# How each stage of a two-layer decoder trunk opens: tile 0 first on four units or a whole chunk, weights split ahead into idle places

## The chip, the cores and the metric

The kernel runs on one core of one Trainium2 chip. The metric is the device time of one execution in microseconds (us). The core has a matrix engine (TensorE, "PE" in the profile, "PEld" for its weight loads), a vector engine (VectorE, "DVE"), a scalar engine (ScalarE, "ACT"), GpSimd ("POOL") and SyncE ("SP", which here only issues the loads of weights and inputs and the stores of the result). Each engine works through its own queue in the order in which the program wrote it, and waits on semaphores for the others. SBUF is the on-chip memory; PSUM is the small memory that TensorE accumulates into.

## The reference

A decoder trunk of two layers on 256 tokens of width 2048, in float32. Cut to what matters:

```
for layer in (0, 1):
    if layer == 0:  q, k, v = split(h @ w_qkv)          # 16 heads of 128, causal, T5 bias
    else:           k, v = split(h @ w_kv); q = h @ w_q # 4 shared K/V heads, window 128, sinks
    attn = softmax(q k^T / sqrt(128) + bias) v @ w_o
    h = layer_norm(sqrt(2) * h + attn)
    u = causal_conv3(h @ w_up) + b                      # 2 x 5504 columns
    g, v = split(u)
    h = layer_norm(sqrt(2) * h + (gelu(g) * v) @ w_down)
```

With 256 tokens the block selection of the first layer leaves plain causal attention. Nearly all the work is the products with weights: 724 weight tiles of 128 x 1024 numbers, each used once.

## The kernel before, in words

**Precision by splitting.** [...] The activations lie in SBUF already split: `xT` holds 16 blocks of 128 features, each with 256 high columns (tokens) and 256 low columns. Weights arrive as float32 ("raw", four buffers, `RAW_BUFS`), one tile of 128 x 1024 at a time, which the code calls a half. `split_upto(i)` (lines 74 to 89) splits all halves up to number i: ACT copies the raw tile to the rounded `wh` (line 85), DVE subtracts to get `wl` (line 86), and the raw buffer is reloaded with the half four further on (`load_weights`, on SP's queue, line 71). The split tiles rotate through four buffers (`spool`, `HALF_BUFS`). `take()` hands the next half to the matmuls, after it has asked for the split of the three halves ahead (`AHEAD`).

**Two ways to multiply.** In `ws_unit` (line 195) the weights are TensorE's stationary operand and all 512 columns of `xT` move: per block of 128 rows one matmul of 512 columns (line 224) and one of 256 (line 227). A unit gives 128 output features for all tokens; it uses two halves. In `Moving` (line 230) the activations are stationary and 512 weight columns move: per block and token tile three matmuls of 512 columns (lines 246 to 248). A chunk gives 512 output columns for both token tiles (tile 0 is tokens 0 to 127, tile 1 the rest).

**Stages.** First attention: V by chunks, Q and K by units, attention per head, and the projection (`project_out`, source `oT`). Then the first feed-forward: 86 units (gate and value feature tiles in turn), a convolution and gate on each pair, and the projection down (`project_out`, source `aT`, 43 blocks a chunk). Then the same for layer 1; its attention begins with one V chunk and four K units. Each `project_out` (line 287) has four chunks of 512 columns; the chunk's sums go to the residual `res` by `evac` (lines 301 and 302, two DVE operations a token tile), queued at the first `take` of the next chunk.

**A stage change.** The next stage needs the normalized residual, turned. In its last 16 blocks (the window, eight halves) a projection works tile by tile (`tilewise`, `late`): all of tile 0 first, then all of tile 1. When tile 0 is complete, DVE evacuates it, takes its moments and normalizes it in four groups of 512 columns (`norm`, lines 317 and 318, two DVE operations a group); while TensorE does tile 1, each group is transposed by TensorE (`turn`, line 327, four transposes), copied by ACT to the high half of `xT` (line 329), and its remainder is written by DVE (`low`, line 334). The window's eight halves have to stay in SBUF for both passes: four in `spool`, and four in `xT`, which is idle then (`aside`). Tile 1 is treated alike, but after the projection's end: the next stage begins meanwhile. A feed-forward begins with one `ws_unit` with `feed`, whose matmuls (lines 208, 209, 213; 256 columns each) start on a block when its turn has been done; the second attention begins with a V chunk whose first eight blocks go tile by tile (`early`).

**Order.** All engines' programs are written out in one order by hand (`manual_schedule`). `at(n, f)` puts f before the matmuls of the n-th step from now, `pe_at` behind them; a step is a half. The framework adds the semaphores.

Of the kernel before, what the change touches and what calls it, by code (L numbers as in the profile page):

```python
# [29 lines left out]
WINDOW = 128  # L30
# [12 lines left out]
WINDOW_BLOCKS = 2 * (HALF_BUFS + SPARE)  # L43


@with_exitstack
def trunk(ctx: ExitStack, tc: tile.TileContext, wst, xT_in, x_in, relb, onehot, umask, sinks, conv_in, ln_g, ln_b, out):
# [13 lines left out]
    todo = {"load": 0, "split": 0}  # L61
# [12 lines left out]
    def split_upto(i):  # L74
        while todo["split"] <= min(i, n_halves - 1):
            s = todo["split"]
            r = raws.pop(s)
            if s in aside:
                j = aside.pop(s)
                wh, wl = (xT[:, k:k + 2, :].rearrange("p a b -> p (a b)") for k in (4 * j, 4 * j + 2))  # L80
            else:
                wh = spool.tile([P, HW], F32R, name="wh")
                wl = spool.tile([P, HW], F32R, name="wl")
            for c in pieces(s):
                nc.scalar.activation(wh[:, c], r[:, c], AF.Copy)  # L85
                nc.vector.tensor_tensor(out=wl[:, c], in0=r[:, c], in1=wh[:, c].bitcast(F32), op=ALU.subtract)  # L86
            halves[s] = (wh, wl)
            todo["split"] += 1
            load_weights()
# [105 lines left out]
    def ws_unit(acc, feed=None):  # L195

        def cols(w, j):
            return w[:, j * P:(j + 1) * P]  # L200

        o = acc[:, 0:T]
        if feed:
            pair = [take(1 - i) for i in range(2)]
            for k in range(KB):
                feed(k)
                wh, wl = pair[k // 8]
                nc.tensor.matmul(o, cols(wh, k % 8), xT[:, k, 0:T], start=(k == 0), stop=False)
                nc.tensor.matmul(o, cols(wl, k % 8), xT[:, k, 0:T], start=False, stop=False)
            feed(KB)  # L210
            split_upto(nexth["i"] + AHEAD - 2)
            for k in range(KB):
                nc.tensor.matmul(o, cols(pair[k // 8][0], k % 8), xT[:, k, T:2 * T], start=False, stop=(k == KB - 1))
                if k % 8 == 7:
                    step()
                    split_upto(nexth["i"] + AHEAD - 2 + (k + 1) // 8)
                    if k < 8:
                        run(before)
            return
        for hf in range(2):  # L220
            wh, wl = take()
            for j in range(8):
                k = hf * 8 + j
                nc.tensor.matmul(acc, cols(wh, j), xT[:, k, :], start=(k == 0), stop=False)  # L224
            for j in range(8):
                k = hf * 8 + j
                nc.tensor.matmul(o, cols(wl, j), xT[:, k, 0:T], start=False, stop=(k == KB - 1))  # L227
            step()

    class Moving:  # L230
# [12 lines left out]
        def mm(self, acc, k, t, wh, wl):  # L243
            sh = self.src[:, k, t * P:(t + 1) * P]
            sl = self.src[:, k, T + t * P:T + (t + 1) * P]
# [20 lines left out]
        def chunk(self, accs, early=None, late=None):  # L266
# [3 lines left out]
            if early:  # L270
                k = 2 * HALF_BUFS
                self.tilewise(accs, 0, k, early)
# [14 lines left out]
    def project_out(src, nk, li, after, preload):  # L287
# [4 lines left out]
        aside.update({w0 + j: j for j in range(SPARE)})  # L292
# [44 lines left out]
        pts = {}  # L337

        def late(t, i):
            last = i == WINDOW_BLOCKS // 2 - 1  # L340
# [6 lines left out]
            if t == 1 and after and i >= SPARE:  # L347
                c = COLS[0][i - SPARE]
                pts[c] = turn(0, c)
                if not last:  # L350
                    low(0, c, pts[c])
                if i < SPARE + 2:
                    split_upto(w0 + WINDOW_BLOCKS // 2 + i - SPARE)
            if t == 1 and last:
                evac(NCH - 1, 1, accs[1])
                sd = moments(1)
                if after:
                    low(0, c, pts[c])
# [5 lines left out]
        for n in range(NCH):  # L364
            accs = [acc_tile(), acc_tile()]
            if n < NCH - 1:
# [71 lines left out]
    def layer_attention(l, rest):  # L438
        with tc.tile_pool(name=f"att{l}", bufs=2) as pool:
            oT = pool.tile([P, NH, 2 * T], F32R, name="oT", bufs=1)  # L440
            bias = pool.tile([P, NH, 2 * P], F32, name="bias", bufs=1)
            if l == 0:
                load_input(pool)
                bias_table(pool)
            else:
                nc.vector.tensor_scalar(nsk, sk, -1.0, None, op0=ALU.mult)
            for i, h in enumerate(range(0, NH, 4)):
                at(4 + (8 - 4 * l) * i, spread_bias, l, h, h + 4)
                at(4 + (8 - 4 * l) * i, load_bias, bias, l, h, h + 4)

            def v_group(early=None):
                mv = Moving(xT, KB)
                accs = [acc_tile(), acc_tile()]
                mv.chunk(accs, early=early)
                vt = pool.tile([P, 2, 512], F32, name="vt", bufs=1 if l else 2)

                def evac():
                    for t in range(2):
                        nc.scalar.activation(vt[:, t, :], accs[t], AF.Copy)

                at(0, evac)
                return vt

            def feat_unit(name, bufs):
                acc = acc_tile()
                ws_unit(acc)
                o = pool.tile([P, T], F32, name=name, bufs=bufs)

                def evac():
                    nc.scalar.activation(o, acc[:, T:2 * T], AF.Copy)  # L470
                    nc.vector.tensor_tensor(out=o, in0=acc[:, 0:T], in1=o, op=ALU.add)

                at(0, evac, first=True)
                return o

            if l == 0:
                for g in range(NH // 4):
                    vt = v_group()
                    for j in range(4):
                        h = 4 * g + j  # L480
                        q = feat_unit("qT", 4)
                        k = feat_unit("kT", 4)
                        attention(pool, l, h, q, vt[:, :, j * P:(j + 1) * P], k, bias, oT)
            else:
                norm, turned = rest
                for i, c in enumerate(COLS[0][:2]):
                    split_upto(nexth["i"] + 2 + i)
                    norm(c)

                def early(t, i):  # L490
                    if i == HALF_BUFS - 1:
                        turn, low = turned
                        pts = [(c, turn(c)) for c in (COLS[0][2:] if t else COLS[0][:2])]
                        for c, pt in pts:
                            low(c, pt)
                        if t == 0:
                            for c in COLS[0][2:]:
                                norm(c)
                    if t:
                        split_upto(nexth["i"] + i)  # L500

                vt = v_group(early)
                ks = [feat_unit("kT", KVH) for _ in range(KVH)]
                for h in range(NH):
                    q = feat_unit("qT", 4)
                    j = h // GRP
                    attention(pool, l, h, q, vt[:, :, j * P:(j + 1) * P], ks[j], bias, oT)
            return project_out(oT, NH, 2 * l, True, AF.Gelu_apprx_tanh)

    def layer_ffn(l, rest):  # L510
        with tc.tile_pool(name=f"ffn{l}", bufs=2) as pool:
            aT = pool.tile([P, FT, 2 * T], F32R, name="aT", bufs=1)
            cw = pool.tile([P, FT, 2, 4], F32, name="cw", bufs=1)
            nc.gpsimd.dma_start(cw, conv_in[l])
            norm, turned = rest
            turn, low = turned
            for c in COLS[1]:
                norm(c)
            pts = {}

            def feed(k):
                for b, c in zip(((0, 0),) + COLS[1], COLS[1]):
                    if k == b[0] and c not in pts:
                        pts[c] = turn(c)
                if k == KB:
                    for c in COLS[1]:
                        low(c, pts[c])

            def conv(i, s, acc, whole, c):
                w = cw[:, i, s, :]  # L530
                h = acc[:, 0:T]
                if not whole:
                    h = pool.tile([P, T], F32, name="h")
                    nc.scalar.activation(h, acc[:, T:2 * T], AF.Copy)
                    nc.vector.tensor_tensor(out=h, in0=acc[:, 0:T], in1=h, op=ALU.add)  # L535
# [115 lines left out]
```

## Time and profile before

| | |
|---|---|
| Median of 3 runs | 2109.02 us (2108.71 to 2109.99) |
| The profiled execution: its own time | 2110.16 us |
| The profiled execution: its span, first to last instruction | 2108.3 us |
| Granted TensorE clock, mean | 0.995 |
| Busy share: PE, DVE, ACT | 99%, 68%, 47% |
| Read from HBM | 401.02 MB, 193 GB/s over the span |

[...] Idle time of an engine other than TensorE costs nothing unless TensorE waits for it. In rows of the timeline the columns are start in us, duration in us, engine, line, operation, output and inputs by name, shape, and in brackets the idle time of the engine ahead of it with what ended it. Groups of instructions have, behind the bar, busy time in us and mean duration in ns, and then the idle time ahead of them.

### The profile page before, as it was taken

The numbers are of one execution on the slowest core, as the hardware profiler recorded it, in microseconds if no ns is written. First come the engines' busy times: TensorE is split into PE (matmuls) and PEld (weight loads), VectorE is DVE, ScalarE is ACT, GpSimd is POOL, SyncE is SP. The second block draws the span as 40 slices with busy tenths as digits, with TensorE's granted clock in tenths as the row PEclk, the third lists the DMA queues.
The fourth block names the chain that finished last, engine by engine and source line by source line (L and its number), as shares of the span: only waits on it lengthen the run. The fifth ranks groups of instructions, "written<-read, shape, count | busy, mean of one in ns | idle before, by whom it ended". The sixth has DMA issues, their size and how long they took to land.

```text
span 2108.3 us, 28513 instructions
## 1 busy us (share of the span) xinstructions
PE 2077.3 (99%) x10962; PEld 1788.2 (85%) x10962; DVE 1434.7 (68%) x2104; ACT 989.1 (47%) x1395; POOL 25.5 (1%) x40
## 2 busy tenths in 40 slices
PE   8999999999999999999999999999999999999997
PEld 7888888888888888888887888888888888888886
DVE  5555555787787787744457676687787778764545
ACT  5444444354545555433344554455555454543342
POOL 1100000000000000000001000000000000000000
PEclk9999999999999999999999999999999999999999
DMA  8855556565555555556666644565555555556663
GB/s 280 299 177 176 171 169 200 183 200 190 190 190 190 188 188 185 189 190 199 192 208 215 210 145 159 181 213 190 189 189 184 191 188 190 190 190 191 194 194 131
DMA packets 114120, 405.08 MB, mean 192 GB/s; under 512 B 15504, under 2 KB 15808, under 8 KB 112704
## 3 DMA queue, kind: packets, MB, share of 16 engines
q1 hardware_dynamic: 106848, 383.83, 56.2%
q0 software_dynamic: 7136, 19.44, 2.6%
q8 instruction: 86, 1.41, 0.3%
q14 instruction: 50, 0.41, 0.1%
HBM read 401.02 MB, written 6.34 MB: 193 GB/s over the span
## 4 chain that ended last, share of the span: by engine, by line
PE 97%; DVE 2%; ACT 0%; issue 0%; DMA 0%; SPq 0%; ACTq 0%; DVEq 0%
PE acc L224 39%; PE acc L227 20%; PE acc L247 12%; PE acc L246 12%; PE acc L248 12%; PE at L388 1%; PE at L421 1%; DVE wl L86 1%; PE at L414 0%; DVE res L317 0%; PE at L387 0%; PE at L422 0%; DVE res L318 0%; DVE xT L334 0%; PE at L327 0%
## 5 line engine op out<-in xcount | busy, mean ns | idle before, releaser
L86 DVE TENSOR_TENSOR wl<-raw,wh 128x1024 fp32r<-128x1024 f32 (+1 forms) x709 | 865.1, 1222 | 595.8 <-ACT wh L85 595.2
L85 ACT ACTIVATE wh<-raw 128x1024 fp32r<-128x1024 f32 (+1 forms) x709 | 750.4, 1059 | 903.7 <-PE acc L248 341.0
L224 PE MATMUL acc<-xT,wh 128*128 128x512 f32 x3552 | 896.3, 394 | 0.0
L224 PEld LDWEIGHTS acc<-xT,wh 128*128 128x128 f32 x3552 | 640.8, 189 | 116.0
L227 PEld LDWEIGHTS acc<-xT,wl 128*128 128x128 f32 x3552 | 484.5, 190 | 34.8
L227 PE MATMUL acc<-xT,wl 128*128 128x256 f32 x3552 | 495.2, 282 | 0.0
L246 PE MATMUL acc<-wh,aT 128*128 128x512 f32 x656 | 255.5, 389 | 0.0
L247 PE MATMUL acc<-wl,aT 128*128 128x512 f32 x656 | 255.2, 389 | 0.0
L248 PE MATMUL acc<-wh,aT 128*128 128x512 f32 x656 | 255.2, 389 | 0.0
L246 PEld LDWEIGHTS acc<-wh,aT 128*128 128x128 f32 x656 | 123.2, 188 | 25.6
L248 PEld LDWEIGHTS acc<-wh,aT 128*128 128x128 f32 x656 | 123.1, 188 | 25.5
L247 PEld LDWEIGHTS acc<-wl,aT 128*128 128x128 f32 x656 | 123.2, 188 | 25.3
L246 PE MATMUL acc<-wh,oT 128*128 128x512 f32 x224 | 88.9, 397 | 0.0
L248 PE MATMUL acc<-wh,oT 128*128 128x512 f32 x224 | 87.3, 390 | 0.0
L247 PE MATMUL acc<-wl,oT 128*128 128x512 f32 x224 | 87.3, 390 | 0.0
L537 DVE SCALAR_TENSOR_TENSOR c<-h,cw,c 128x255 f32<-128x255 f32 x170 | 82.3, 484 | 6.0
L538 DVE SCALAR_TENSOR_TENSOR c<-h,cw,c 128x254 f32<-128x254 f32 x170 | 82.2, 484 | 6.1
L536 DVE TENSOR_SCALAR c<-h,cw 128x256 f32<-128x256 f32 x170 | 70.1, 412 | 6.1
L246 PE MATMUL acc<-wh,xT 128*128 128x512 f32 x160 | 65.7, 411 | 8.7 <-ACT wh L85 8.5
L535 DVE TENSOR_TENSOR h<-acc,h 128x256 f32<-128x256 f32 x170 | 70.9, 417 | 0.0
L544 ACT ACTIVATE aT<-c 128x256 fp32r<-128x256 f32 x86 | 36.0, 418 | 69.7 <-DVE c L541 69.7
L247 PE MATMUL acc<-wl,xT 128*128 128x512 f32 x160 | 63.8, 399 | 1.7 <-DVE wl L86 1.7
(102 smaller groups left out, 1191.5 us busy)
## 6 DMA issues: line engine op xcount, KB each, us to landing
raw<-in_wst_dram SPq DMA_DIRECT2D x723, 512.0 KB, 3.4
band<-ud POOLq DMA_DIRECT2D x8, 512.0 KB, 13.3
bias<-band POOLq DMA_DIRECT2D x8, 512.0 KB, 5.3
gb<-in_ln_g_dram POOLq DMA_DIRECT2D x4, 1024.0 KB, 6.0
gb<-in_ln_b_dram POOLq DMA_DIRECT2D x4, 1024.0 KB, 9.3
res<-in_x_dram POOLq DMA_DIRECT2D x2, 1024.0 KB, 10.8
out_dram<-res SPq DMA_DIRECT2D x8, 256.0 KB, 2.5
xc<-in_xT_dram SPq DMA_DIRECT2D x7, 256.0 KB, 7.3
```

The costliest lines, as they stand in the source:

```text
L85: nc.scalar.activation(wh[:, c], r[:, c], AF.Copy)
L86: nc.vector.tensor_tensor(out=wl[:, c], in0=r[:, c], in1=wh[:, c].bitcast(F32), op=ALU.subtract)
L224: nc.tensor.matmul(acc, cols(wh, j), xT[:, k, :], start=(k == 0), stop=False)
L227: nc.tensor.matmul(o, cols(wl, j), xT[:, k, 0:T], start=False, stop=(k == KB - 1))
L246: nc.tensor.matmul(acc, sh, wh, start=(k == 0), stop=False)
L247: nc.tensor.matmul(acc, sh, wl, start=False, stop=False)
L248: nc.tensor.matmul(acc, sl, wh, start=False, stop=(k == self.nk - 1))
L535: nc.vector.tensor_tensor(out=h, in0=acc[:, 0:T], in1=h, op=ALU.add)
L536: nc.vector.tensor_scalar(c, h, w[:, 2:3], w[:, 3:4], op0=ALU.mult, op1=ALU.add)
L537: nc.vector.scalar_tensor_tensor(c[:, 1:T], h[:, 0:T - 1], w[:, 1:2], c[:, 1:T], op0=ALU.mult, op1=ALU.add)
L538: nc.vector.scalar_tensor_tensor(c[:, 2:T], h[:, 0:T - 2], w[:, 0:1], c[:, 2:T], op0=ALU.mult, op1=ALU.add)
L544: nc.scalar.activation(aT[:, i, 0:T], g, AF.Copy)
```

## The change

1. **Opening of a feed-forward.** `ws_unit` with `feed` is replaced by `ws_opening` on four units. It first does the high part of the weights on token tile 0 alone, for all four units one after another (each matmul moves two runs of 128 columns: tile 0's high and low columns of one block), then the same for tile 1 in groups of four blocks across the four units, and last the low parts of the weights on both tiles. `between` puts the normalization, turning and low parts of tile 1 in between.
2. **Opening of the second attention.** The V chunk goes tile by tile over all 16 blocks, not eight. It is put ahead of the new stage's buffers (`stage`), and so are its steps ahead of the loads of the layer's bias, which begin after it.
3. **Weights split ahead.** The eight halves of the next stage's opening are to be split by then. Idle places are used beside `xT`: for the attention projections, blocks of the coming feed-forward's buffer (`up`), and for the first down-projection, blocks of its own source that are no longer read. The attention's output and the first 16 blocks of the feed-forward's activations now share one permanent buffer (`st`), so that `up` can be reserved from the projection's second chunk on (`turnover`). The last four halves of the window, and the halves 4 to 7 of the next stage, go to those places. `reach` makes `take` ask for splits further ahead, from 19 halves before the window (`RAMP`).
4. **The split in two steps.** `high_upto` does ACT's copies alone; `split_upto` follows with DVE's part. Two halves of the next stage get their high part during tile 1's pass and their low part later.
5. **In the window** the turns of tile 0 come after the halves 3 to 6 of tile 1's pass, where they came after 4 to 7.

The last projection, with nothing behind it, keeps its order.

```diff
+WINDOW = WINDOW_BLOCKS // 2
+OPENING = 4
+RAMP = 19
...
     def take(ahead=AHEAD):
         i = nexth["i"]
         nexth["i"] += 1
-        split_upto(i + ahead)
+        split_upto(max(i + ahead, reach.get(i, 0)))
         run(before)
...
+    st = big.tile([P, NH, 2 * T], F32R, name="st")
...
+    def ws_opening(accs, between, done):
+        n0 = nexth["i"]
+        nexth["i"] += 2 * len(accs)
+        run(before)
+        pair = [[halves.pop(n0 + 2 * u + i) for i in range(2)] for u in range(len(accs))]
+
+        def high(u, t, ks):
+            part = lambda a: a.rearrange("p (s t c) -> p s t c", s=2, t=2)[:, :, t, :]
+            for k in ks:
+                nc.tensor.matmul(part(accs[u]), cols(pair[u][k // 8][0], k % 8), part(xT[:, k, :]),
+                                 start=(t == 0 and k == 0), stop=False)
+
+        for u in range(len(accs)):
+            between(u)
+            high(u, 0, range(KB))
+        for c in range(KB // 4):
+            between(len(accs) + c)
+            for u in range(len(accs)):
+                high(u, 1, range(4 * c, 4 * c + 4))
+        for u, acc in enumerate(accs):
+            for k in range(KB):
+                nc.tensor.matmul(acc[:, 0:T], cols(pair[u][k // 8][1], k % 8), xT[:, k, 0:T],
+                                 start=False, stop=(k == KB - 1))
+            step()
+            step()
+            done(u)
+            run(before)
...
             if early:
-                k = 2 * HALF_BUFS
+                k = WINDOW_BLOCKS
                 self.tilewise(accs, 0, k, early)
...
-    def project_out(src, nk, li, after, preload):
+    def project_out(src, nk, li, homes, preload, turnover=None):
         mv = Moving(src, nk)
         w0 = nexth["i"] + (nk * NCH - WINDOW_BLOCKS) // 2
-        aside.update({w0 + j: j for j in range(SPARE)})
+        n0 = w0 + WINDOW
+        aside.update({w0 + j: (xT, j) for j in range(SPARE)})
+        after = homes is not None
+
+        def settle():
+            h = homes()
+            aside.update({w0 + SPARE + j: h[j] for j in range(4)})
+            aside.update({n0 + 4: h[4], n0 + 5: h[5], n0 + 6: h[0], n0 + 7: h[1]})
+            for m in range(RAMP + 3):
+                i = w0 - RAMP + m
+                cap = w0 + SPARE + 3 if i < w0 - 3 else i + 11
+                reach[i] = min(i + AHEAD + m // 2, cap)
...
-            if t == 1 and after and i >= SPARE:
-                c = COLS[0][i - SPARE]
-                pts[c] = turn(0, c)
-                if not last:
-                    low(0, c, pts[c])
-                if i < SPARE + 2:
-                    split_upto(w0 + WINDOW_BLOCKS // 2 + i - SPARE)
+            if t == 1 and after:
+                if 3 <= i < 7:
+                    c = COLS[0][i - 3]
+                    low(0, c, turn(0, c))
+                if 5 <= i < 7:
+                    high_upto(n0 + i + 1)
...
         for n in range(NCH):
             accs = [acc_tile(), acc_tile()]
+            if n == 1 and turnover:
+                turnover()
+            if n == 1 and after:
+                settle()
...
+            for c in cc[:3]:
+                norm(c)
+            def between(i):
+                if i == OPENING - 1:
+                    low(cc[0], turn(cc[0]))
+                    norm(cc[3])
+                if OPENING <= i < OPENING + 3:
+                    c = cc[i - OPENING + 1]
+                    low(c, turn(c))
+                    if i > OPENING:
+                        split_upto(n0 + i + 1)
```

The opening of the second attention, in the new version:

```
            norm(c[0])
            norm(c[1])
            split_upto(n0 + 7)
            norm(c[2])

            def early(t, i):
                if t == 0 and i == 5:
                    pts = [turn(c[j]) for j in range(2)]
                    low(c[0], pts[0])
                    norm(c[3])
                    low(c[1], pts[1])
                if t == 0 and i == 7:
                    low(c[2], turn(c[2]))
                if t == 1 and i == 1:
                    low(c[3], turn(c[3]))
                if t == 1 and i < HALF_BUFS:
                    split_upto(n0 + 8 + i)
```

More of the change, by code (lines that the diff above doesn't have):

```diff
@@ L29 @@
 MAXD = 128
-WINDOW = 128
+SWA = 128
 ALPHA = math.sqrt(2.0)
@@ L60, in trunk @@
     raws, halves, aside = {}, {}, {}
-    todo = {"load": 0, "split": 0}
+    todo = {"load": 0, "high": 0, "low": 0}
+    reach, placed = {}, {}
     def pieces(u):
@@ L83, in split_upto, with low_piece @@
                 wl = spool.tile([P, HW], F32R, name="wl")
+            halves[s] = placed[s] = (wh, wl)
             for c in pieces(s):
[L85 to L88, printed above, removed]
+                nc.scalar.activation(wh[:, c], raws[s][:, c], AF.Copy)
+                if len(pieces(s)) > 1:
+                    low_piece(s, c)
+            todo["high"] += 1
+    def low_piece(s, c):
+        wh, wl = placed[s]
+        nc.vector.tensor_tensor(out=wl[:, c], in0=raws[s][:, c], in1=wh[:, c].bitcast(F32), op=ALU.subtract)
+    def split_upto(i):
+        while todo["low"] <= min(i, n_halves - 1):
+            s = todo["low"]
+            high_upto(s)
+            if len(pieces(s)) == 1:
+                low_piece(s, slice(0, HW))
+            raws.pop(s), placed.pop(s)
+            todo["low"] += 1
             load_weights()
@@ L193, in load_bias, with cols, ws_unit @@
         nc.gpsimd.dma_start(bias[:, h0:h1, :], band[l, h0:h1].rearrange("h q j -> q h j"))
-    def ws_unit(acc, feed=None):
-        def cols(w, j):
-            return w[:, j * P:(j + 1) * P]
+    def cols(w, j):
+        return w[:, j * P:(j + 1) * P]
+    def ws_unit(acc):
         o = acc[:, 0:T]
[L203 to L219, printed above, removed]
         for hf in range(2):
@@ L436, in attention @@
         at(5, outputs)
[L438 to L508, printed above, removed]
@@ new lines, in trunk, with __init__, __call__, homes @@
+    class FeedForward:
+        def __init__(self, l, stage):
+            self.l, self.stage = l, stage
+        def __call__(self):
+            self.pool = pool = self.stage(f"ffn{self.l}")
+            self.up = pool.tile([P, FT - NH, 2 * T], F32R, name="up", bufs=1)
+            self.cw = pool.tile([P, FT, 2, 4], F32, name="cw", bufs=1)
+            nc.gpsimd.dma_start(self.cw, conv_in[self.l])
+        def homes(self):
+            return [(self.up, j) for j in range(6)]
+        def block(self, k):
+            return st[:, k, :] if k < NH else self.up[:, k - NH, :]
+        def run(self, rest):
+            l, pool = self.l, self.pool
+            norm, (turn, low) = rest
+            n0 = nexth["i"]
+            cc = COLS[1]
+            for c in cc[:3]:
+                norm(c)
+            def between(i):
[7 more added lines that the diff above has]
+                        split_upto(n0 + i + 1)
+            def conv(i, s, acc, c):
+                w = self.cw[:, i, s, :]
+                h = pool.tile([P, T], F32, name="h")
+                nc.scalar.activation(h, acc[:, T:2 * T], AF.Copy)
+                nc.vector.tensor_tensor(out=h, in0=acc[:, 0:T], in1=h, op=ALU.add)
@@ L558, in layer_ffn, with after @@
-            return project_out(aT, FT, 2 * l + 1, l == 0, AF.Exp)
-    rest = None
-    for l in range(2):
-        rest = layer_ffn(l, layer_attention(l, rest))
+                b = self.block(i)
+                nc.scalar.activation(b[:, 0:T], g, AF.Copy)
+                nc.vector.tensor_tensor(out=b[:, T:2 * T], in0=g, in1=b[:, 0:T].bitcast(F32), op=ALU.subtract)
+            cs = {}
+            def after(u, acc):
+                i, s = divmod(u, 2)
+                cs[s] = pool.tile([P, T], F32, name=f"c{s}")
+                at(0, conv, i, s, acc, cs[s])
+                if s == 0:
+                    at(1, nc.scalar.activation, cs[0], cs[0], AF.Gelu_apprx_tanh)
+                else:
+                    at(0, gate, i, cs[0], cs[1])
+                    at(1, store, i, cs[0])
@@ new lines, in run, with opened @@
+            accs = [acc_tile() for _ in range(OPENING)]
+            def opened(u):
+                after(u, accs[u])
+                if u < 2:
+                    split_upto(n0 + 2 * OPENING + 2 * u + 1)
+            ws_opening(accs, between, opened)
+            for u in range(OPENING, 2 * FT):
+                acc = acc_tile()
+                ws_unit(acc)
+                after(u, acc)
+            homes = None
+            if l == 0:
+                homes = lambda: [(st, j) for j in range(4)] + [(self.up, j) for j in range(2)]
@@ L565, in _bucket, with stage @@
+            return project_out(self.block, FT, 2 * l + 1, homes, AF.Exp)
+    with ExitStack() as held:
+        def stage(name):
+            held.close()
+            return held.enter_context(tc.tile_pool(name=name, bufs=2))
+        rest = None
+        for l in range(2):
+            ff = FeedForward(l, stage)
+            rest = ff.run(layer_attention(l, rest, stage, ff))
 def _bucket(d):
```

112 lines of the change are left out of this document (65 added, 47 removed).

## The prediction

> **What bounds the kernel now.** The page first.
>
> ```profile
> span 2108.3 us, 28513 instructions
> PE 2077.3 (99%) x10962; PEld 1788.2 (85%) x10962; DVE 1434.7 (68%) x2104; ACT 989.1 (47%) x1395; POOL 25.5 (1%) x40
> L86 DVE TENSOR_TENSOR wl<-raw,wh 128x1024 fp32r<-128x1024 f32 (+1 forms) x709 | 865.1, 1222 | 595.8 <-ACT wh L85 595.2
> raw<-in_wst_dram SPq DMA_DIRECT2D x723, 512.0 KB, 3.4
> band<-ud POOLq DMA_DIRECT2D x8, 512.0 KB, 13.3
> bias<-band POOLq DMA_DIRECT2D x8, 512.0 KB, 5.3
> ```
>
> TensorE is busy 99% of the span, so only its holes can be won. The view of waits, for TensorE, says where they are:
>
> ```profile
> PE acc L246 <- ACT wh L85: 8.5, 2, 7.0
> PE at L327 <- DVE res L318: 4.8, 3, 3.6
> PE at L327 <- issue: 3.6, 1, 3.6
> PE acc L247 <- DVE wl L86: 1.7, 2, 0.9
> ```
>
> 7.0 us of it is the first load of the kernel, which stays. All the rest lies at the three stage changes: A (first attention to first feed-forward), B (feed-forward to second attention), C (second attention to second feed-forward). TensorE's timeline there, first A, then C, then B (start, us, instruction):
>
> ```profile
> 386.66 0.60 PE L327 MATMUL at<-ident,res 128*128 128x128 f32 x4
> ...
> 387.33 0.40 PE L247 MATMUL acc<-wl,oT 128*128 128x512 f32 x1
> ...
> 392.15 0.60 PE L327 MATMUL at<-ident,res 128*128 128x128 f32 x4
> 396.30 1.08 PE L327 MATMUL at<-ident,res 128*128 128x128 f32 x4 [3.56 <-issue]
> ...
> 398.90 0.41 PE L209 MATMUL acc<-xT,wl 128*128 128x256 f32 x1
> 399.11 0.41 PE L208 MATMUL acc<-xT,wh 128*128 128x256 f32 x1
> ...
> 406.85 2.00 PE L224 MATMUL acc<-xT,wh 128*128 128x512 f32 x8
> 408.69 1.11 PE L227 MATMUL acc<-xT,wl 128*128 128x256 f32 x8
> 409.64 2.00 PE L224 MATMUL acc<-xT,wh 128*128 128x512 f32 x8
> ```
>
> ```profile
> 1373.27 0.60 PE L327 MATMUL at<-ident,res 128*128 128x128 f32 x4
> ...
> 1387.28 2.00 PE L224 MATMUL acc<-xT,wh 128*128 128x512 f32 x8
> ```
>
> ```profile
> 1111.59 0.60 PE L327 MATMUL at<-ident,res 128*128 128x128 f32 x4
> ...
> 1117.43 0.49 PE L246 MATMUL acc<-wh,xT 128*128 128x512 f32 x1
> ...
> 1146.43 1.98 PE L224 MATMUL acc<-xT,wh 128*128 128x512 f32 x8
> ```
>
> Durations overlap, so prices are distances of starts: 512 columns 1.84/8 = 0.23 us, 256 columns 0.95/8 = 0.12, one turn of four transposes 387.33 - 386.66 - 0.23 = 0.44. What A loses: from 392.15 to 406.85 are 14.70 us for five turns (2.20) and 48 matmuls of 256 (5.76), so 6.7 lost. C: 14.01 - 7.96 = 6.05. B: 29.00 from 1117.43 to 1146.43, for 96 matmuls (22.1) and four turns (1.76), so 5.2. Together 18.0 us, 0.85% of the time: the most that the change can win. In A 3.56 is idle; behind it 256 columns take 0.21 (398.90 to 399.11), not 0.12: the clock has dropped. Of the 12.8 us of A and C, 3.6 and 4.8 are those idle waits; the other 4.4, 2.2 a change, are the low clock and restarts.
>
> **The change part by part.** I call a weight tile of 128x1024 a half, w0 to w0+7 the eight halves of the last window of a projection, n0 onward those of the next stage; "high" is ACT's copy (L85), "low" DVE's subtraction (L86).
>
> *What fills the holes.* After tile 1's last matmul the next stage runs 64 matmuls of 256 columns in A and C (7.7 us), or 48 of 512 in B (11 us), on tile 0 alone. From the rows below, DVE needs 3.7 us from the start of an evacuation to the first normalized columns and 1.5 for each further group. Means of the turn's other two steps:
>
> ```profile
> L334 DVE TENSOR_TENSOR xT<-at,xT 128x512 fp32r<-128x512 f32 x24 | 15.9, 677 | 3.3 <-ACT xT L329 3.3
> ...
> L329 ACT ACTIVATE xT<-at 128x512 fp32r<-128x512 f32 x24 | 14.1, 598 | 36.8 <-PE at L327 36.8
> ```
>
> In A, counted from tile 1's end, three groups are normalized at 4.1, 5.6 and 7.1, the fourth behind a low at 9.3. TensorE turns the first at 5.8 (three units of 16 x 0.12), ends the fourth unit at 8.1, turns the second, and then alternates 16 matmuls and a turn: the last turn ends at 13.3, its low at 13.3 + 0.60 + 0.68 = 14.6, and its matmuls are due at 15.2. That is the tightest place: 0.6 of cover, and beyond it A pays one for one. In B the first turn comes at 8.3 (six halves of 1.38). No stall there, so the 18.0 would go.
>
> *What the opening costs.* Four units of 48 matmuls at 0.12 instead of one such and three of 5.60 (409.64 - 406.85 = 2.79 a half): 3 x 0.16 = 0.5 us each in A and C. The operand in two runs of 128 columns is not in the trace. Below: nothing. Above: two passes of the 128-wide kind, a quarter turn (0.11) each, so 0.22: 128 x 0.10 = 12.5 us an opening. I take 0.12, the row with the same column count. The first unit now copies before its convolution, as all others do: off TensorE's path.
>
> *What the weights split ahead cost: the term that decides.* Fourteen splits (w0 to n0+5) are put ahead of the end of tile 0's pass, where eight were, and DVE works in program order. So tile 0's evacuation, its normalization, and the turns that TensorE waits for stand behind the low of n0+5. The earlier start (19 halves ahead) does not help: up to w0-1 the splits go to four rotating buffers and wait for TensorE. Only from w0 on can they run free, and then the four raw buffers set the pace, since each reload (on SP's queue) waits for the low that frees its buffer. A's rows, ACT and then DVE:
>
> ```profile
> 363.34 1.28 ACT L371 ACT_TABLE_LOAD   x1
> ...
> 365.12 1.06 ACT L85 ACTIVATE xT<-raw 128x1024 fp32r<-128x1024 f32 x1 [0.29 <-DMA raw<-in_wst_dram]
> ...
> 371.94 1.06 ACT L85 ACTIVATE wh<-raw 128x1024 fp32r<-128x1024 f32 x1 [0.45 <-DMA raw<-in_wst_dram]
> ```
>
> ```profile
> 360.53 2.35 DVE L86 TENSOR_TENSOR xT<-raw,xT 128x1024 fp32r<-128x1024 f32 x2
> ...
> 368.50 0.69 DVE L301 SCALAR_TENSOR_TENSOR res<-res,acc 128x512 f32<-128x512 f32 x1 [1.05 <-PE acc L248]
> ...
> 371.15 4.62 DVE L86 TENSOR_TENSOR wl<-raw,wh 128x1024 fp32r<-128x1024 f32 x4
> 380.06 0.69 DVE L301 SCALAR_TENSOR_TENSOR res<-res,acc 128x512 f32<-128x512 f32 x1 [4.29 <-PE acc L248]
> ...
> 383.01 0.75 DVE L318 SCALAR_TENSOR_TENSOR res<-res,rs,gb 128x512 f32<-128x512 f32 x1
> ```
>
> w0+3 to w0+7 start at 365.12 to 371.94, ended by DMA waits: 1.70 us a half. Evacuating a chunk takes 371.15 - 368.50 = 2.65. Now A after the change. The extra reach puts chunk 1's evacuation behind w0's low (361.7): DVE goes on at 364.4, w0+1's low ends at 365.6, and only then is the raw of w0+5 loaded. It lands 3.4 later (the page); high at 369.1. Five more at 1.70: n0+2 at 377.6, done 378.7. On ACT the table load (1.28, and 0.2 for its activation) comes next, so n0+3 runs from 380.2 to 381.2, its low to 382.4. Chunk 2's evacuation, queued behind that low, runs to 385.1; n0+4 and n0+5, long landed, take 2.3: tile 0's evacuation starts at 387.4 instead of 380.06. First group ready 3.70 later (380.06 to 383.01 + 0.75): 391.1. TensorE wants it after the fourth half, one half (1.38) ahead of today's 386.66: 385.3. **A stall of 5.8 us**, longer than today's 3.56, and behind it the low clock, mostly inside tile 1's pass: of the 2.2 of today I take 2.0, since one restart falls away (bounds 0 and 2.2). C has the same code: the same.
>
> Bounds of that stall: DVE without a late load needs 5.3 for two evacuations and 13 x 1.16 for lows behind 361.7, so 382.1 and 0.5 us. At the slowest landing seen around A,
>
> ```profile
> DMA to landing us min/median/max: 3.4/4.6/5.7
> ```
>
> a buffer's round is 5.7 + 1.06 + 1.22 + 0.2 = 8.2, 2.05 a half: n0+2 at 381.7, everything 4.0 later, 9.8 us. I take 5.8, since 1.70 was measured at this place.
>
> B lacks two of these: chunks there have 21.5 halves, so chunk 2's evacuation and the table load pass long before the window.
>
> ```profile
> 1089.87 1.06 ACT L85 ACTIVATE xT<-raw 128x1024 fp32r<-128x1024 f32 x1 [1.74 <-DMA raw<-in_wst_dram]
> ...
> 1096.80 1.06 ACT L85 ACTIVATE wh<-raw 128x1024 fp32r<-128x1024 f32 x1 [1.11 <-DMA raw<-in_wst_dram]
> ```
>
> ```profile
> 1104.98 0.69 DVE L301 SCALAR_TENSOR_TENSOR res<-res,acc 128x512 f32<-128x512 f32 x1 [5.87 <-PE acc L248]
> ...
> 1107.94 0.75 DVE L318 SCALAR_TENSOR_TENSOR res<-res,rs,gb 128x512 f32<-128x512 f32 x1
> ```
>
> w0+7's high starts at 1096.80; six more at 6.93/4 = 1.73: n0+5 at 1107.2, low done 1109.5. First group 3.71 later: 1113.2, wanted at 1111.59 - 1.38 = 1110.2: a stall of 3.0 (0 to 4.9 by the same bounds). That is between gaps after which the clock held (1.5 at most in B) and those after which it fell: I take 0.8 of the 2.0.
>
> [...]
>
> *Queues.* The bias and band loads of layer 1 start behind B's chunk; their first use is 11 halves (31 us) later against 13.3 + 5.3: hidden, with 12 us to spare. The convolution weights go onto POOL's queue earlier: hidden.
>
> *Sum*, against the profiled execution (2110.16, 1.1 above the median): A 5.8 + 2.0 + 0.5 - 6.7 = +1.6; C 8.3 - 6.05 = +2.25; B 3.0 + 0.8 - 5.2 = -1.4. **+2.4 us**, put on the median of 2109.02: **2111.4**. Anything within 0.2% (4.2 us) cannot be told from no change.
>
> **The rivals.**
> - *The change does what it says* (faster): lows are done before tile 0's pass ends. For it: DVE is idle 4.29 us ahead of 380.06. Against: DVE alone is 2 us late in A. 2109.0 - 18.0 + 1.0 = 2092.0.
> - *Loads come faster than 1.70.* The best stretch in the view of windows:
>
> ```profile
> 410.00:415.00 5.00, 5.00 (x31) 4.37 (x30) 1.91 (x4) 1.36 (x2) 0.00 (x0) 1.00 0.89 357
> ```
>
> At 357 GB/s a half of 0.524 MB takes 1.47: n0+2 in A 1.2 earlier (stall 4.6), n0+5 in B 1.6 earlier (1.4, clock kept). +0.4 + 1.0 - 3.8 = -2.4: 2106.6. Against it: it wants four loads always under way, and a buffer is with ACT and DVE for 2.3 us of its round. [...]
> - *Loads come slower* (slower): 2.05 a half, because the ring never rests. Stalls of 9.8, 9.8 and 4.9, the clock falling in all: +5.6 + 6.2 + 1.7 = +13.5, 2122.5. It decides from about 1.8 us a half on (one tenth more moves a stall by 1.1 in A). For it: landings up to 5.7.
> - *The two-run operand costs double* (slower): 2111.4 + 25 = 2136. Against: the column count is the same.
>
> **How the numbers follow.** Likeliest 0.50 (own range 2106 to 2117), full gain 0.12, faster loads 0.18, slower loads 0.15, operand 0.05. Below 2104.8: 0.12, a third of the faster loads (0.06), a little of the first (0.02): 0.20. Above 2113.2: 0.20 and a quarter of the likeliest (0.13): 0.33. Between: 0.47. The range leaves out the full gain, the operand and a little of the slower loads: 2103 to 2124.
>
> **What would show it.** Right: TensorE idle some 5 us in the middle of tile 1's pass in A and C, ended by the normalization; DVE's evacuation of tile 0 about 7 us behind its pass, right behind two lows; 3 us in B; no wait in the openings. Wrong: no wait of a turn in that pass, or DVE idle ahead of tile 0's evacuation (the full gain); waits between the opening's matmuls (tile 1's chain mis-sized); starts over 0.12 apart in the opening (the operand); loads of the window at another pace than 1.7.

## The result, and the profile after

| | before | after |
|---|---|---|
| Median (lowest to highest) of 20 runs each | 2109.96 us (2108.69 to 2112.18) | 2113.75 us (2111.24 to 2115.58) |
| Ratio, 95% interval | | 1.0017, 1.0010 to 1.0023 |
| The profiled execution, its span | 2110.16, 2108.3 us | 2114.11, 2112.3 us |

The changed kernel is slower by 3.8 us (ratio 1.0017): with 20 runs each the interval excludes no change, although the size is below the 0.2% that the prediction named as the least that can be told from none. Forecast were 2111.4, that is 2.4 more than before, and a range of 2103 to 2124.

The page of the changed kernel first:

```profile
span 2112.3 us, 28688 instructions
PE 2078.3 (98%) x11058; PEld 1793.6 (85%) x11058; DVE 1437.4 (68%) x2106; ACT 989.8 (47%) x1397; POOL 25.5 (1%) x40
PE 94%; DVE 2%; DMA 2%; ACT 1%; issue 0%; SPq 0%; ACTq 0%; DVEq 0%
```

The busy times of PE, DVE and ACT are those of before within 3 us, and the third line, the chain that ended last, is TensorE's for 94%. So the 4.0 us that the span has grown are to be looked for in TensorE's waits and in its clock, and the view of waits for TensorE has only three lines:

```profile
PE at L376 <- DVE res L367: 15.5, 3, 6.2
PE acc L279 <- ACT wh L92: 6.2, 1, 6.2
PE acc L280 <- DVE wl L99: 0.2, 1, 0.2
```

The second is the kernel's first load, as before. All waits of the old openings are gone. In their place the turns of tile 0 (`at`, line 376) wait for the normalization (line 367) three times, once at each stage change, for 15.5 us. Stage change A in the timeline, first ACT, then DVE, then TensorE:

```profile
369.24 1.06 ACT L92 ACTIVATE up<-raw 128x1024 fp32r<-128x1024 f32 x1 [1.97 <-DMA raw<-in_wst_dram]
...
377.58 1.06 ACT L92 ACTIVATE wh<-raw 128x1024 fp32r<-128x1024 f32 x1 [0.37 <-DMA raw<-in_wst_dram]
378.66 1.28 ACT L419 ACT_TABLE_LOAD   x1
...
382.91 1.06 ACT L92 ACTIVATE up<-raw 128x1024 fp32r<-128x1024 f32 x1 [0.55 <-DMA raw<-in_wst_dram]
```

```profile
361.39 0.68 DVE L350 SCALAR_TENSOR_TENSOR res<-res,acc 128x512 f32<-128x512 f32 x1
...
382.28 0.68 DVE L350 SCALAR_TENSOR_TENSOR res<-res,acc 128x512 f32<-128x512 f32 x1
...
384.92 2.34 DVE L99 TENSOR_TENSOR up<-raw,up 128x1024 fp32r<-128x1024 f32 x2
387.18 0.68 DVE L350 SCALAR_TENSOR_TENSOR res<-res,acc 128x512 f32<-128x512 f32 x1
...
390.13 0.75 DVE L367 SCALAR_TENSOR_TENSOR res<-res,rs,gb 128x512 f32<-128x512 f32 x1
```

```profile
384.79 0.39 PE L281 MATMUL acc<-xT,st 128*128 128x512 f32 x1
390.94 1.12 PE L376 MATMUL at<-ident,res 128*128 128x128 f32 x4 [5.75 <-DVE res L367]
...
400.13 4.00 PE L244 MATMUL acc<-xT,wh 128*128 128x256 f32 x32
403.97 2.08 PE L244 MATMUL acc<-xT,up 128*128 128x256 f32 x16
...
424.91 2.00 PE L226 MATMUL acc<-xT,wh 128*128 128x512 f32 x8
```

Read them from the bottom up. TensorE stands for 5.75 us until the normalized group of 390.13 + 0.75. DVE had begun tile 0's evacuation at 387.18 only, directly behind the two lows of n0+4 and n0+5 (384.92), and those behind chunk 2's evacuation (382.28), which is the place in DVE's program that the prediction described. The copies that feed DVE run at the pace of the loads: six of them start from 369.24 to 377.58, each after a wait for its load, (377.58 - 369.24)/5 = 1.67 us a half.

The other two changes, B and then C:

```profile
1115.17 1.12 PE L376 MATMUL at<-ident,res 128*128 128x128 f32 x4 [3.49 <-DVE res L367]
...
1367.53 0.39 PE L281 MATMUL acc<-xT,st 128*128 128x512 f32 x1
1374.15 1.12 PE L376 MATMUL at<-ident,res 128*128 128x128 f32 x4 [6.23 <-DVE res L367]
...
1408.04 2.00 PE L226 MATMUL acc<-xT,wh 128*128 128x512 f32 x8
```

And the view of windows, A and then B. In each row: the stretch and its length in us, the busy time of PE, PEld, DVE, ACT and POOL with their instructions, the granted clock, the DMA share and GB/s:

```profile
384.66:388.07 3.41, 0.52 (x3) 0.10 (x1) 3.38 (x5) 0.00 (x0) 0.00 (x0) 1.00 0.53 159
388.07:391.48 3.41, 0.54 (x3) 0.55 (x4) 2.98 (x6) 0.29 (x1) 0.00 (x0) 0.50 0.66 246
391.48:394.89 3.41, 3.41 (x12) 2.72 (x11) 3.30 (x6) 0.60 (x1) 0.00 (x0) 0.50 0.00 0
...
1111.70:1115.11 3.41, 0.00 (x0) 0.00 (x0) 2.94 (x7) 0.29 (x1) 0.00 (x0) 1.00 0.77 263
1115.11:1118.52 3.41, 3.35 (x10) 2.79 (x11) 3.34 (x6) 0.60 (x1) 0.00 (x0) 0.50 0.07 24
1118.52:1121.93 3.41, 3.41 (x20) 2.85 (x19) 2.29 (x5) 1.41 (x3) 0.00 (x0) 1.00 0.00 0
```

The clock is at half for one whole busy stretch of 3.41 us in each (the second low stretch in A, the only one in B): 1.7 us lost, since half the work gets done (10 to 12 matmuls and turns there, 19 to 20 in the next stretch).

By the prediction's own method A loses 424.91 - 384.79 = 40.12, less one start (0.23), 24 matmuls of 512 columns (5.52), eight turns (3.52) and 192 matmuls of 256 (23.04): 7.8, and 0.5 for the opening, 8.3. C, from 1367.53 to 1408.04, loses 40.51 less the same: 8.2, and 0.5: 8.7. B has 3.49 and 1.7: 5.2. Against the losses before (6.7, 6.05, 5.2) that is +1.6, +2.65 and 0: +4.25, where the span has grown by 4.0 and the median by 3.8.

### The profile page after: what moved, and what is told of

It reads as the page before. It is cut to its first block, busy times and chain, and to the rows that moved or that the text cites. A ratio compares the mean times of both kernels' runs of the same rounds, so it can differ in the third digit from the quotient of the medians.

```text
span 2112.3 us, 28688 instructions
## 1 busy us (share of the span) xinstructions
PE 2078.3 (98%) x11058; PEld 1793.6 (85%) x11058; DVE 1437.4 (68%) x2106; ACT 989.8 (47%) x1397; POOL 25.5 (1%) x40
## 4 chain that ended last, share of the span: by engine, by line
PE 94%; DVE 2%; DMA 2%; ACT 1%; issue 0%; SPq 0%; ACTq 0%; DVEq 0%
PE acc L226 38%; PE acc L229 19%; PE acc L279 11%; PE acc L280 11%; PE acc L281 11%; DMA raw<-in_wst_dram 2%; PE acc L244 1%; PE acc L256 1%; PE at L436 1%; PE at L469 1%; PE at L376 1%; PE at L462 0%; ACT wh L92 0%; DVE xT L99 0%; DVE up L99 0%
## 5 line engine op out<-in xcount | busy, mean ns | idle before, releaser
L99 DVE TENSOR_TENSOR wl<-raw,wh 128x1024 fp32r<-128x1024 f32 (+1 forms) x685 | 836.6, 1222 | 592.7 <-ACT wh L92 587.4
L92 ACT ACTIVATE wh<-raw 128x1024 fp32r<-128x1024 f32 (+1 forms) x685 | 725.0, 1059 | 867.1 <-PE acc L281 334.9
L279 PE MATMUL acc<-wh,st 128*128 128x512 f32 x448 | 175.5, 392 | 0.0
L281 PE MATMUL acc<-wh,st 128*128 128x512 f32 x448 | 174.4, 389 | 0.0
L280 PE MATMUL acc<-wl,st 128*128 128x512 f32 x448 | 174.3, 389 | 0.0
L279 PE MATMUL acc<-wh,up 128*128 128x512 f32 x384 | 149.4, 389 | 0.0
L280 PE MATMUL acc<-wl,up 128*128 128x512 f32 x384 | 149.4, 389 | 0.0
L281 PE MATMUL acc<-wh,up 128*128 128x512 f32 x384 | 149.4, 389 | 0.0
L281 PEld LDWEIGHTS acc<-wh,st 128*128 128x128 f32 x448 | 84.1, 188 | 17.8
L279 PEld LDWEIGHTS acc<-wh,st 128*128 128x128 f32 x448 | 84.1, 188 | 17.1
L280 PEld LDWEIGHTS acc<-wl,st 128*128 128x128 f32 x448 | 84.2, 188 | 17.0
L279 PEld LDWEIGHTS acc<-wh,up 128*128 128x128 f32 x384 | 72.1, 188 | 15.0
L281 PEld LDWEIGHTS acc<-wh,up 128*128 128x128 f32 x384 | 72.1, 188 | 15.0
L280 PEld LDWEIGHTS acc<-wl,up 128*128 128x128 f32 x384 | 72.1, 188 | 14.8
```

What stands on the lines that cost most here:

```text
L92: nc.scalar.activation(wh[:, c], raws[s][:, c], AF.Copy)
L99: nc.vector.tensor_tensor(out=wl[:, c], in0=raws[s][:, c], in1=wh[:, c].bitcast(F32), op=ALU.subtract)
L279: nc.tensor.matmul(acc, sh, wh, start=(k == 0), stop=False)
L280: nc.tensor.matmul(acc, sh, wl, start=False, stop=False)
L281: nc.tensor.matmul(acc, sl, wh, start=False, stop=(k == self.nk - 1))
```

## The experiments

The theory: the number of halves of the next stage whose low is queued on DVE ahead of tile 0's evacuation sets the stall, at the pace of the loads; nothing else in the change costs. Rivals: the early start of the extra splits (`RAMP`), which pushes chunk evacuations back, is the cause; the bare openings cost something of their own, so that the gain wouldn't come even without the stall.

**The ramp taken away.** The far reach begins at the window's first half, not 19 halves earlier, and is asked for behind the evacuation:

```diff
-        split_upto(max(i + ahead, reach.get(i, 0)))
+        split_upto(i + ahead)
         run(before)
+        split_upto(reach.get(i, 0))
...
-            for m in range(RAMP + 3):
+            for m in range(RAMP, RAMP + 3):
```

> The changed kernel, but nothing is split further ahead than before the change until the window begins (the reach starts at w0, not 19 halves earlier), and the evacuation of a finished chunk stands ahead of the extra splits. Theory (the four raw buffers set the pace of the splits): the evacuations go back to their old places but the last split, n0+5, still ends near 386.9, so tile 0's evacuation moves by under 1 us and the stalls in A and C stay at 5 to 6 us; time as the changed kernel, within 0.1%. Rival (the evacuations queued behind the splits are the cause): tile 0's evacuation starts 5.3 us earlier, the stalls in A and C shrink to about 0.5 and the clock stays up: about 2099 us. Rival (the early reach gives the splits a lead): without it the stalls grow by several us each, over 2118 us.

Measured: 2112.71 us (11 runs) against 2110.6 for the kernel before, ratio 1.0011 (1.0002 to 1.0019). Waits, then DVE's timeline:

```profile
PE at L377 <- DVE res L368: 13.5, 3, 5.4
```

```profile
368.10 0.69 DVE L351 SCALAR_TENSOR_TENSOR res<-res,acc 128x512 f32<-128x512 f32 x1 [1.26 <-PE acc L282]
...
386.48 0.68 DVE L351 SCALAR_TENSOR_TENSOR res<-res,acc 128x512 f32<-128x512 f32 x1
```

A chunk's evacuation is back near its old place (368.10 after an idle wait for TensorE, 368.50 before the change), and tile 0's evacuation comes at 386.48 instead of 387.18. The three stalls are 2.0 us shorter together (13.5 for 15.5). So the ramp, and the order of the chunk evacuations that the prediction followed through step by step, is worth 0.7 us of A's delay; the rest is elsewhere. Nor did the stalls grow, as they would have if the ramp gave the splits a lead. The two intervals overlap, so the time by itself doesn't show even that.

**Fewer halves ahead.** For the next three kernels I rewrote the order around the change so that the number of the last half ahead of tile 0's evacuation is a constant (`PRE`, for projections of 16 and of 43 blocks): the others follow between the turns of tile 1's pass, ACT's copies first. The table load moves behind the last turn and tile 1's groups are normalized one or two ahead of their turns (neither is in the lines below), and there is no ramp.

```diff
-RAMP = 19
+PRE = {16: 1, 43: 3}
...
-            for m in range(RAMP + 3):
-                i = w0 - RAMP + m
-                cap = w0 + SPARE + 3 if i < w0 - 3 else i + 11
-                reach[i] = min(i + AHEAD + m // 2, cap)
+            pre = PRE[nk]
+            reach.update({w0 + 5: n0 + min(0, pre), w0 + 6: n0 + min(1, pre), w0 + 7: n0 + pre})
...
+                if i < 3:
+                    high_upto(n0 + min(max(pre + 1 + i, 2), 5))
                 if 3 <= i < 7:
                     c = COLS[0][i - 3]
                     low(0, c, turn(0, c))
-                if 5 <= i < 7:
+                if i == 3:
+                    split_upto(n0 + (2 if nk == 16 else 4))
+                if i == 4:
+                    high_upto(n0 + 5)
+                if i == 5:
+                    split_upto(n0 + (3 if nk == 16 else 5))
+                if 5 <= i < 7 and nk > 16:
                     high_upto(n0 + i + 1)
```

The kernel with n0+1 as the last ahead in A and C, n0+3 in B:

> The changed kernel's openings, but in DVE's order only the lows up to n0+1 (A, C) or n0+3 (B) stand ahead of tile 0's evacuation; ACT still makes the highs of the later halves during tile 1's pass, and their lows come behind tile 0's normalization and in the opening. Theory (what stands ahead of tile 0's evacuation on DVE is the whole cause): no stall in tile 1's pass, clock up throughout, and the 18 us of the stage changes go but for 0.5 in each opening of a feed-forward: about 2093 us (2091 to 2097). Rival (the openings themselves lose time, by their tile 1 chain or the two-run operand): new waits between the opening's matmuls, over 2100 us.

The same with n0+3 everywhere (`PRE = {16: 3, 43: 3}`):

> As the kernel with one (A, C) or three (B) lows ahead, but with the lows up to n0+3 ahead of tile 0's evacuation in A and C too. Theory: in A the low of n0+3 ends near 383.3, so the first normalized group is ready at 387.0 where TensorE wants it at 385.3: a stall of 1.7 us in A and in C, the clock kept: some 3.4 us over that kernel. Rival (two more splits are free, cover is there): the same time.

The same with n0+5 everywhere, as in the change (`PRE = {16: 5, 43: 5}`):

> The same kernel with all lows up to n0+5 ahead of tile 0's evacuation, as in the changed kernel, but without its early reach and with its other steps in the new order. Theory: stalls of 5 to 6 us in A and C, 3 to 3.5 in B, each followed by a stretch at half clock: 2110 to 2114 us, no better than the kernel before. Rival (the new order of the other steps is what helps): well under 2105 us.

| Last half ahead in A and C | us | Ratio to before (95%) | Start of tile 0's evacuation in A | Stalls A, B, C, us |
|---|---|---|---|---|
| n0+1 (B: n0+3) | 2097.69 | 0.9939 (0.9926 to 0.9951) | 380.16 | none |
| n0+3 (B: n0+3) | 2101.42 | 0.9958 (0.9944 to 0.9971) | 383.24 | 1.84, none, 2.05 |
| n0+5 (B: n0+5) | 2112.81 | 1.0009 (1.0001 to 1.0018) | 386.66 | 5.56, 2.92, 5.35 |

The rows of DVE's timeline with that start, in the same order (the first with the low ahead of it):

```profile
379.01 1.22 DVE L99 TENSOR_TENSOR wl<-raw,wh 128x1024 fp32r<-128x1024 f32 x1 [1.32 <-ACT wh L92]
380.16 0.68 DVE L348 SCALAR_TENSOR_TENSOR res<-res,acc 128x512 f32<-128x512 f32 x1
```

```profile
383.24 0.68 DVE L348 SCALAR_TENSOR_TENSOR res<-res,acc 128x512 f32<-128x512 f32 x1
```

```profile
386.66 0.68 DVE L348 SCALAR_TENSOR_TENSOR res<-res,acc 128x512 f32<-128x512 f32 x1
```

and the waits of the second and the third:

```profile
PE at L374 <- DVE res L365: 3.9, 2, 2.0
```

```profile
PE at L374 <- DVE res L365: 13.8, 3, 5.6
```

Two halves more move the evacuation by 3.08 and by 3.42, 1.54 and 1.71 a half: the pace of the loads. With n0+5 ahead the rewritten order is as slow as the change itself, although ramp, table load and tile 1's order are other ones; so these are not the cause. With n0+1 all three stalls are gone, and the time falls 12.9 us below the kernel before. The theory stands, for the size too: from n0+5 to n0+1 are 15.1 us in time, of which 13.8 are stalls that the profile shows, and the rest is low clock less what became late in their place. Two details missed: with n0+3 the clock was expected to hold, and behind C's stall it fell (the last section has the rows); and 2097.69 lies just above the 2091 to 2097 that were expected for n0+1. What became late shows in the waits of that kernel:

```profile
PE acc L226 <- DVE h L619: 2.4, 2, 1.7
...
PE acc L229 <- DVE wl L99: 0.5, 1, 0.5
PE acc L226 <- ACT wh L92: 0.3, 1, 0.3
```

The fifth unit needs an accumulator that the first unit's convolution (`h`, line 619) has to read first; and that convolution is queued on DVE behind the lows of two halves that have just been loaded. The kernel with n0+5 ahead has no such wait.

**The convolution first.** The n0+1 kernel, with the first units' convolutions put ahead of the two splits:

```diff
             def opened(u):
                 after(u, accs[u])
+                run(before)
                 if u < 2:
                     split_upto(n0 + 2 * OPENING + 2 * u + 1)
```

> The kernel with one (A, C) or three (B) lows ahead, and one more change: when a unit of the opening is complete, its convolution stands ahead of the two next splits, so that its PSUM tile is free earlier. In that kernel TensorE waits 1.7 us ahead of the fifth unit in A and 0.7 in C for the first unit's sum to be taken out of PSUM (DVE did two lows first, late because of late loads), and 0.8 us for late splits two units on in A. Theory: these waits go, 2 to 3 us: about 2095 us. Rival (the late loads beside the 2 MB of gamma and beta and the band are what counts): the wait moves to the splits and the time stays within 1 us of that kernel.

Measured: 2093.19 us (2093.05 to 2093.72, five runs) against 2110.29, ratio 0.9920 (0.9907 to 0.9934). Its page and its waits of TensorE, all of them:

```profile
span 2091.3 us, 28691 instructions
PE 2072.1 (99%) x11058; PEld 1789.0 (86%) x11058; DVE 1435.5 (69%) x2106; ACT 987.8 (47%) x1397; POOL 25.5 (1%) x40
```

```profile
PE acc L279 <- ACT wh L92: 6.2, 2, 5.7
PE acc L280 <- DVE wl L99: 0.8, 1, 0.8
```

Both lines are the kernel's start. The view has no wait at a stage change any more, and the span is 17.0 us shorter than before. This is the time that the prediction gave its rival "the change does what it says" (2092.0 from 2109.0: 18.0 less 1.0 for two openings). So the second rival theory falls: the openings cost about what was put down for them. This kernel beats both the one before and the changed one. Set against the kernel before, measured beside each of the two (2110.6 and 2110.29), this kernel gains 4.2 us on the n0+1 kernel, more than the 2 to 3 that were expected; the waits listed there were 3.2.

**B alone with n0+5 ahead.** The n0+1 kernel, with `PRE = {16: 1, 43: 5}`:

> The kernel with one (A, C) or three (B) lows ahead, but in B all lows up to n0+5 ahead of tile 0's evacuation, so that only B stalls. Theory: a stall of 2.9 us in B, and behind it a whole clock window of 3.4 us at half rate (1.7 to 1.8 us more): 4.5 to 5 us over that kernel, 2102.5. [...]

Measured: 2101.64 us (2099.41 to 2102.2, five runs), ratio 0.9957 (0.9944 to 0.9969): 8.65 below the kernel before, where the n0+1 kernel was 12.9 below it. The five runs lie in two groups, 2099.4 and 2099.6, and 2101.6 to 2102.2. The profiled one is of the lower (2099.58), 10.7 below the kernel before and so 2.2 above the n0+1 kernel. Its wait and its windows:

```profile
PE at L374 <- DVE res L365: 2.2, 1, 2.2
```

```profile
1104.10:1107.52 3.42, 2.76 (x13) 1.95 (x11) 2.94 (x6) 0.31 (x2) 0.00 (x0) 1.00 0.90 314
1107.52:1110.93 3.41, 1.89 (x11) 1.59 (x12) 3.34 (x6) 0.60 (x1) 0.00 (x0) 1.00 0.46 153
1110.93:1114.34 3.41, 3.41 (x20) 2.89 (x19) 3.34 (x6) 1.50 (x3) 0.00 (x0) 1.00 0.00 0
```

A stall of 2.18, and the clock held (1.00 in all three rows): the 2.2 us are the stall alone. It is shorter than the 2.9 that was expected, and the stretch at half rate expected behind it isn't there. The upper group lies some 2.5 above the lower, more than the price of one low stretch (1.7). That the clock fell in those runs isn't shown, since none of them has a profile, and the mean clock on record for each run (0.997 for these three, 0.998 and 0.997 for the other two) can't settle it, since it contains the low clock of the kernel's tail as well (0.50 from 2090.60 on in the profiled execution). That the clock makes the two groups is the author's estimate, from the stalls of this size in the last section, one of them with a low row behind it.

## Why the prediction was right, and where it was off

- *Where the change is decided: right.* The weights split ahead, in DVE's order, make tile 0's evacuation late. Forecast for A were n0+2's copy at 377.6 (measured 377.58), the evacuation at 387.4 (387.18), a stall of 5.8 (5.75), 1.70 us a half (1.67), and the low clock at 2.0 (7.8 - 5.75 = 2.1 in A, 8.2 - 6.23 = 2.0 in C). The three kernels with n0+1, n0+3 and n0+5 ahead show that this is the cause, not only that it stands in the same place.
- *A step of the chain with less weight than told.* Much of the working went into chunk evacuations that the ramp displaces. They were displaced as described (361.39, 382.28), but without the ramp tile 0's evacuation still starts at 386.48. The loads set the pace either way; n0+5's own copy still waited for its load (382.91, 0.55 idle), where the prediction had it "long landed".
- *A mean taken for each of two, without effect.* The 3.6 and 4.8 of idle wait in the prediction are two lines of the view of waits, not the two stages: by the timeline before, A had 3.56 + 0.41 = 3.97 and C 3.60 + 0.82 = 4.42. So its 2.2 a change for low clock and restarts is the mean of 2.7 in A and 1.6 in C; the sum is the same.
- *The opening: right.* 32 matmuls on the operand in two runs of 128 columns take 403.97 - 400.13 = 3.84, 0.12 each, as taken; twice that is excluded (128 x 0.10 is 12.8 rather than 12.5 us; nothing hangs on it). No wait stands in the openings of the changed kernel, but the cover behind them was thin: in the kernels with n0+1 and n0+3 ahead the fifth unit waited for a convolution. The prediction put that step down as "off TensorE's path", and it was so only with n0+5 ahead. In the other two the opening begins earlier, and the lows that free the raw buffers of n0+4 and n0+5 come later (with n0+1 ahead at 404.66 and 407.01, in the changed kernel from 384.92); which of the two counts was not separated.
- *C: the stall was 0.4 short.* It was taken as A's, 5.8; it was 6.23. The loads were slower there: the copies of w0+5 to n0+2 start from 1351.32 to 1360.45, 1.83 us a half.
- *B: the mis-sized term.* The prediction's "3.0 + 0.8" for stall and clock was 3.49 + 1.7. The copies from w0+7 to n0+5 (1097.98 to 1109.18) came 1.87 us apart, where 1.73 was taken. The 0.8 was a middle between a clock that holds and one that falls; the profiled execution paid a whole low stretch (0.50 from 1115.11 to 1118.52). So B's forecast gain of 1.4 was none. B's 1.4 and C's 0.4 are what lies between the +2.4 that were forecast and the +4.25 counted in the timeline (+3.8 in the medians).
- *The rivals.* Faster loads than 1.70 (2106.6) are out by the measured 1.67, 1.83 and 1.87. Slower ones at 2.05 (2122.5) are out as well, though B and C went some of that way. The full gain was out by the three waits, but its price was right: it came (2093.19) once the halves ahead were four fewer in A and C, two fewer in B, and a convolution went first, in the rewritten order.

## What to carry to other kernels

Work put ahead into "idle places" of an in-order engine isn't in an idle place if it waits for a load: everything behind it then runs at the pace of the loads, here 1.5 to 1.7 us for each half ahead of the evacuation in A. Count what is queued between the late load and the instruction that the bottleneck engine needs, and move only as much ahead as has landed by then; the rest can follow behind the critical step. When the stall goes, look at once for what was covered by it (here a convolution behind two splits, worth 4.2 us).

## What the runs showed of the hardware

**Behind a stall of 2.05 us the clock fell, behind one of 2.18 it didn't.** The kernel with n0+3 ahead shows, for A's stall of 1.84 and then C's of 2.05, in rows as long as B's low stretch in the changed kernel (3.41 us, 1115.11 to 1118.52):

```profile
382.53:385.94 3.41, 2.62 (x12) 1.85 (x10) 2.98 (x6) 0.96 (x2) 0.00 (x0) 1.00 0.79 259
385.94:389.35 3.41, 2.36 (x15) 2.05 (x16) 3.31 (x6) 1.83 (x3) 0.00 (x0) 1.00 0.25 99
...
1358.73:1362.14 3.41, 1.40 (x7) 0.82 (x5) 2.94 (x7) 1.98 (x3) 0.00 (x0) 1.00 0.96 322
1362.14:1365.55 3.41, 3.37 (x10) 2.79 (x11) 3.34 (x5) 0.81 (x2) 0.00 (x0) 0.50 0.02 6
```

C's stall lies in one row, TensorE was busy for 1.40 of its 3.41 us, and the next row has half the clock. A's lies in two rows, with 2.62 and 2.36 busy, and both have 1.00. In the last experiment the 2.18 lie in two rows as well, the worse has 1.89 busy (1107.52 above), and the row behind it has 1.00. So of these three stalls of about 2 us, one has a low row behind it (0.50 for 3.41 us, about 1.7 us more by the loss counted above), and it is not the longest of them: its length alone doesn't decide, and what does isn't settled here.

**Weight loads took 7.1 us while POOL's queue loaded too, 4.4 where it didn't.** In the n0+1 kernel, gamma, beta and the attention's band are loaded while the next stage opens. DMA issues from 404 to 424, KB each and median us from issue to landing:

```profile
raw<-in_wst_dram SPq DMA_DIRECT2D x8, 512.0 KB, 7.1
gb<-in_ln_g_dram POOLq DMA_DIRECT2D x1, 1024.0 KB, 4.8
gb<-in_ln_b_dram POOLq DMA_DIRECT2D x1, 1024.0 KB, 8.8
band<-ud POOLq DMA_DIRECT2D x1, 512.0 KB, 16.7
```

A weight load takes 7.1 there; over the whole of the changed kernel it is 3.3, and in a stretch where the weight loads follow each other as closely without the other queue (13 from 360 to 384 in the changed kernel) it was 4.4. It comes together with the late lows ahead of the convolution in that kernel; that POOL's loads are the cause isn't shown, since no other place for them was tried.
